# The last part of the first gate is computed before the queries instead of after the third branch projection

## The chip, the cores and the metric

One core of a Trainium2 chip runs the whole program once. The time is device microseconds (us) of one execution; the figure compared is the median of several runs of the same program. TensorE (PE) multiplies matrices into PSUM banks, VectorE (DVE) and ScalarE (ACT) read and write those banks and SBUF, GpSimd (POOL) does a few small things, and SyncE (SP) issues nearly all transfers from HBM, in one row, each waiting for its buffer.

## What is computed

A transformer block and then a second, two-layer block, on 256 tokens of width 2048. The part that the change touches is the mixing stage of the first block:

```python
mod = (c @ w_mod[l] + b_mod[l]).reshape(B, N_MOD, D)
shift_m, scale_m, gate_m = mod[:, 0, None], mod[:, 1, None], mod[:, 2, None]
...
proj = h @ w_in[l]
y_a = gmlp_spatial_gating(proj[..., COL_UV:COL_QLAT], ...)
q = apply_rope((q_lat @ w_q_up[l]).reshape(B, S, ATTN_HEADS, HEAD_DIM), cos_a, sin_a)
...
y_b = dsa_attention(q, k, v, q_idx, k_idx, idx_w)
gates = jax.nn.sigmoid(proj[..., COL_GATE:])
merged = gates[..., :D] * (y_a @ w_proj_a[l]) + gates[..., D:] * (y_b @ w_proj_b[l])
mix_out = merged @ w_out[l]
x = x + gate_m * rms_norm(mix_out, g_post_mix[l])
```

## The kernel before

Weights come in pieces of 1 MB (128 partitions x 2048 floats, tile `raw`, three buffers). Each piece is split in two halves of 1024 columns, and each half into a rounded part `wh` (line 134, ACT) and the rest `wl` (line 135, DVE), three buffers each. Every product is made of three matmuls (`mm3`; lines 144 to 146, or 211 to 213 in `linT`). A superblock of 512 output columns is 16 blocks of 128 input rows for the big weights, so four pieces. It takes two PSUM banks out of a ring of four (`acca`); the next superblock but one takes the same banks again and waits until DVE and ACT have read them.

The mixing stage runs jobs in the order of the string `ORDER`: `G` and `g` are superblocks of the first gate (tanh on ACT), `k` keys, `v` values, `S` the spatial gating, `Q` the queries, `A` starts the attention, `p0` to `p3` the four superblocks of the first branch projection, which multiply the gate by the projected branch. Behind them, outside the string, come four rounds of second gate (`w_in_g2`, four pieces) and second branch projection (`w_pb`, two pieces), and then the output projection `w_out` (function `post`, four superblocks of four pieces, `linT`).

Two kinds of side work are spread over the weight pieces. At the end of every piece `side()` runs:

```python
self.due += self.rate
while self.due >= 1 and todo:
    self.due -= 1
    self.mod_tile(new, *todo.pop(0))
for _ in range(self.pace):
    next(self.work, None)
```

`mod_tile` loads one 512 KB tile of `w_mod` (`rawm`, three buffers, line 453, issued by SP) and adds it into a running sum (`mac`, line 460, DVE). There are 96 such tiles; after each 16 a group of eight small matmuls (line 442) turns the sum into 8 columns of `mods`. `rate` is set by `r3` and `r4` in the string and is 0 ahead of `r3`. The first two groups give `gate_m`; their product with a gain, `Gm`, is turned into a row: a PE transposition (line 269), a copy on ACT (271), a store to HBM on POOL's queue (272, `grow`) and two loads that spread it over 128 partitions (275, `gr`). `work` is the attention, one head per `next`: scores (line 1024, PE), mask (1027, DVE), maximum (1043, DVE), exponentials (1044, ACT), reciprocal (1045, DVE), scaling (1047, ACT), transpositions (1054, PE), values (1030 to 1032, PE).

In `post`, each superblock's banks are released by a square on ACT (line 252) and by the product with the spread row, on DVE:

```python
done = self.nc.vector.tensor_mul(mix[h][:, c * 512:(c + 1) * 512], banks[h][q], G(c))   # line 930
```

The queries' banks are released by the rotary embedding: two copies on ACT (346, 347) and a product on DVE (350, `qT`). A scheduler turns this program into one fixed row of instructions for each engine; each engine then works through its row in order.

Of the kernel before, what the change touches and what calls it, by code (L numbers as in the profile page):

```python
# [28 lines left out]
SCALE = 128.0 ** -0.5  # L29


ORDER = "m2 m3 m4 G2 g9 g10 k0 k1 v7 v8 S r3 Q A r4 p0 p1 p2 G3 p3"

PACE = (3, 1)

# [54 lines left out]
class Kern:  # L90
# [380 lines left out]
    def block1(self, c1):  # L471
# [174 lines left out]
        def attend():  # L646
# [4 lines left out]
                "S": spatial, "Q": queries, "A": attend}  # L651
        for j in ORDER.split():
            if j[0] == "r":
# [819 lines left out]
```

## Time and profile before

| | |
|---|---|
| median of 3 runs | 2440.88 us (2440.26 to 2445.6) |
| the profiled execution | 2438.1 us, of which its span 2436.1 us |
| PE busy | 2378.1 us, 98% of the span |
| DVE busy | 1678.5 us, 69% |
| mean granted clock of PE | 0.991 |
| transfers | 540.61 MB, 222 GB/s over the span |

Busy times are sums over the whole program; they hide stages in which another engine is full. What a stage can gain or lose is read from where PE stands idle, and from what ended that idle time.

### The profile page before, as it was taken

The numbers are of one execution on the slowest core, as the hardware profiler recorded it, in microseconds if no ns is written. First come the engines' busy times: TensorE is split into PE (matmuls) and PEld (weight loads), VectorE is DVE, ScalarE is ACT, GpSimd is POOL, SyncE is SP. The second block draws the span as 40 slices with busy tenths as digits, with TensorE's granted clock in tenths as the row PEclk, the third lists the DMA queues.
The fourth block names the chain that finished last, engine by engine and source line by source line (L and its number), as shares of the span: only waits on it lengthen the run. The fifth ranks groups of instructions, "written<-read, shape, count | busy, mean of one in ns | idle before, by whom it ended". The sixth has DMA issues, their size and how long they took to land.

```text
span 2436.1 us, 37172 instructions
## 1 busy us (share of the span) xinstructions
PE 2378.1 (98%) x15142; PEld 2153.9 (88%) x15142; DVE 1678.5 (69%) x2213; ACT 1246.7 (51%) x1716; POOL 19.3 (1%) x30
## 2 busy tenths in 40 slices
PE   7999999999989999999999989999999999999997
PEld 6899989999868888888888879998898899999986
DVE  8997898888777575555556566756664477777764
ACT  5877674534464444444445454445644455554543
POOL 0000000000000000000000000000000000000000
PEclk9999999999999999999999999999999999999999
DMA  9997557999948585555555545555655544454453
GB/s 365 349 365 259 182 177 272 329 350 333 350 161 321 191 291 193 190 189 187 194 197 200 190 149 191 191 189 186 228 193 190 190 163 167 158 189 169 161 190 138
DMA packets 104043, 540.61 MB, mean 222 GB/s; under 512 B 9888, under 2 KB 18240, under 8 KB 53184
## 3 DMA queue, kind: packets, MB, share of 16 engines
q1 hardware_dynamic: 100896, 526.19, 60.8%
q10 hardware_dynamic: 2160, 8.88, 1.0%
q0 software_dynamic: 816, 3.16, 0.4%
q8 instruction: 118, 1.93, 0.3%
q14 instruction: 53, 0.43, 0.1%
HBM read 533.99 MB, written 4.21 MB: 221 GB/s over the span
## 4 chain that ended last, share of the span: by engine, by line
PE 94%; DVE 2%; ACT 1%; DMA 1%; issue 1%; POOL 0%; SPq 0%; DVEq 0%; POOLq 0%
PE acca L145 15%; PE acca L144 15%; PE acca L146 15%; PE acca L212 11%; PE acca L211 11%; PE acca L213 11%; PE acca L193 2%; PE acca L194 2%; PE acca L192 2%; PE accb L212 2%; PE accb L213 2%; PE accb L211 2%; DMA hid<-in_w_mod_dram 1%; DVE wl L135 1%; PE accb L1343 1%
## 5 line engine op out<-in xcount | busy, mean ns | idle before, releaser
L135 DVE TENSOR_TENSOR wl<-raw,wh 128x1024 fp32r<-128x1024 f32 x802 | 977.9, 1221 | 570.9 <-ACT wh L134 568.3
L134 ACT CAST wh<-raw 128x1024 fp32r<-128x1024 f32 x802 | 841.7, 1051 | 864.0 <-PE acca L213 377.9
L145 PE MATMUL acca<-Ql,wh 128*128 128x256 f32 x1024 | 290.5, 284 | 0.0
L144 PE MATMUL acca<-Qh,wh 128*128 128x256 f32 x1024 | 289.8, 284 | 0.0
L146 PE MATMUL acca<-Qh,wl 128*128 128x256 f32 x1024 | 285.5, 281 | 0.0
L212 PE MATMUL acca<-wl,Fh 128*128 128x512 f32 x704 | 276.8, 393 | 1.0 <-DVE wl L135 0.9
L213 PE MATMUL acca<-wh,Fl 128*128 128x512 f32 x704 | 275.7, 393 | 0.3 <-DVE Fl L716 0.3
L211 PE MATMUL acca<-wh,Fh 128*128 128x512 f32 x704 | 252.3, 396 | 1.7 <-ACT Fh L714 1.7
L144 PE MATMUL acca<-xh,wh 128*128 128x256 f32 x832 | 232.8, 284 | 4.5 <-ACT xh L808 3.4
L145 PE MATMUL acca<-xl,wh 128*128 128x256 f32 x832 | 233.7, 284 | 0.0
L146 PE MATMUL acca<-xh,wl 128*128 128x256 f32 x832 | 227.0, 283 | 0.0
L144 PEld LDWEIGHTS acca<-Qh,wh 128*128 128x128 f32 x1024 | 192.9, 188 | 0.5
L145 PEld LDWEIGHTS acca<-Ql,wh 128*128 128x128 f32 x1024 | 192.6, 188 | 0.8
L146 PEld LDWEIGHTS acca<-Qh,wl 128*128 128x128 f32 x1024 | 192.1, 189 | 0.4
L144 PEld LDWEIGHTS acca<-xh,wh 128*128 128x128 f32 x832 | 158.1, 190 | 7.3 <-ACT xh L808 3.6
L145 PEld LDWEIGHTS acca<-xl,wh 128*128 128x128 f32 x832 | 157.4, 189 | 1.6 <-issue 0.7
L212 PEld LDWEIGHTS acca<-wl,Fh 128*128 128x128 f32 x704 | 132.7, 189 | 29.1 <-DVE wl L135 2.2
L211 PEld LDWEIGHTS acca<-wh,Fh 128*128 128x128 f32 x704 | 131.3, 188 | 30.0 <-ACT Fh L714 2.9
L213 PEld LDWEIGHTS acca<-wh,Fl 128*128 128x128 f32 x704 | 132.4, 188 | 28.6 <-DVE Fl L716 1.5
L146 PEld LDWEIGHTS acca<-xh,wl 128*128 128x128 f32 x832 | 155.1, 190 | 1.3 <-issue 1.0
L145 PE MATMUL acca<-Al,wh 128*128 128x256 f32 x512 | 143.7, 282 | 0.0
L144 PE MATMUL acca<-Ah,wh 128*128 128x256 f32 x512 | 142.7, 281 | 0.0
(374 smaller groups left out, 4600.5 us busy)
## 6 DMA issues: line engine op xcount, KB each, us to landing
raw<-in_w_fgu_dram SPq DMA_DIRECT2D x88, 1024.0 KB, 4.8
raw<-in_w_inb_dram SPq DMA_DIRECT2D x64, 1024.0 KB, 4.8
raw<-in_w_in_dram SPq DMA_DIRECT2D x51, 1024.0 KB, 6.3
rawm<-in_w_mod_dram SPq DMA_DIRECT2D x96, 512.0 KB, 5.7
raw<-in_w_fd_dram SPq DMA_DIRECT2D x44, 1024.0 KB, 4.8
raw<-in_w_ina_dram SPq DMA_DIRECT2D x32, 1024.0 KB, 4.8
raws<-in_w_mod_dram SPq DMA_DIRECT2D x30, 1024.0 KB, 8.4
raw<-in_w_in_g_dram SPq DMA_DIRECT2D x16, 1024.0 KB, 7.2
```

What stands on the lines that cost most here:

```text
L134: nc.scalar.copy(wh[:, :per], raw[:, a:a + per])
L135: nc.vector.tensor_sub(wl[:, :per], raw[:, a:a + per], wh[:, :per].bitcast(F32))
L144: mm(out, ah, bh, start=start, stop=False, skip_group_check=True)
L145: mm(out, ah, bl, start=False, stop=False, skip_group_check=True)
L146: mm(out, al, bh, start=False, stop=stop, skip_group_check=True)
L192: mm(banks[h], xh[:, t], wh[:, s], start=fresh and k == 0, stop=False, skip_group_check=True)
L193: mm(banks[h], xh[:, t], wl[:, s], start=False, stop=False, skip_group_check=True)
L194: mm(banks[h], xl[:, t], wh[:, s], start=False, stop=k == nk - 1, skip_group_check=True)
L211: mm(banks[h][q], xh[:, t], wh[:, w], start=k == 0, stop=False, skip_group_check=True)
L212: mm(banks[h][q], xh[:, t], wl[:, w], start=False, stop=False, skip_group_check=True)
L213: mm(banks[h][q], xl[:, t], wh[:, w], start=False, stop=k == nk - 1, skip_group_check=True)
L1343: nc.tensor.matmul(ps[:, g * T:(g + 1) * T], q[g][:, P:T], kT, start=g == 0, stop=g == 1, skip_group_check=True)
```

## The change

One job of the order string moves: `G3`, the last superblock of the first gate (four pieces, 192 matmuls of 256 columns), from behind `p2` to behind `S`. No instruction is added or removed.

```diff
-ORDER = "m2 m3 m4 G2 g9 g10 k0 k1 v7 v8 S r3 Q A r4 p0 p1 p2 G3 p3"
+ORDER = "m2 m3 m4 G2 g9 g10 k0 k1 v7 v8 S G3 r3 Q A r4 p0 p1 p2 p3"
```

What else moves follows from the string: `G3` now stands where `rate` is 0 and no attention is running. Before, its four pieces had `rate` 4 and one head each.

**Behind the queries, DVE.** `wl` are weight halves, `yal` the rest of the gated branch, `qT<-acca` releases a queries' bank. Before:

```order
L135 TENSOR_TENSOR wl<-raw,wh 128x1024
L351 TENSOR_TENSOR sw<-sw,sinr 128x512
L337 TENSOR_TENSOR yal<-sv,yah 128x512
L135 TENSOR_TENSOR wl<-raw,wh 128x1024
L1096 SCALAR_TENSOR_TENSOR sv<-sv,u 128x512
L460 SCALAR_TENSOR_TENSOR mac<-rawm,vec,mac 128x1024
L350 TENSOR_TENSOR qT<-acca,cosr 128x512 x3
```

DVE at the same work now:

```order
L1096 SCALAR_TENSOR_TENSOR sv<-sv,u 128x512 x2
L135 TENSOR_TENSOR wl<-raw,wh 128x1024
L337 TENSOR_TENSOR yal<-sv,yah 128x512 x2
L135 TENSOR_TENSOR wl<-raw,wh 128x1024 x5
L350 TENSOR_TENSOR qT<-acca,cosr 128x512
L351 TENSOR_TENSOR sw<-sw,sinr 128x512
L135 TENSOR_TENSOR wl<-raw,wh 128x1024
L352 TENSOR_TENSOR qT<-qT,sw 128x512
L350 TENSOR_TENSOR qT<-acca,cosr 128x512
```

The rest of the spatial gating (`sv`, `yal`) and the tile sum (line 460) no longer stand among or right ahead of the releases.

**In the output projection, PE.** `acca_6710` and `acca_6711` are the banks of its first superblock, `acca_6858` and `acca_6859` of its second, `acca_7002` of its third, which is the ring's first pair again. Before:

```order
L211 MATMUL acca_6711<-wh_6816,xh_93 128x512
L442 MATMUL accb_5529<-cst_84,rawm_5522 128x1 x8
L269 MATMUL accb_6695<-cst_84,Gm_89 16x128
L212 MATMUL acca_6710<-wl_6817,xh_93 128x512
...
L211 MATMUL acca_6858<-wh_6862,xh_93 128x512
...
L211 MATMUL acca_7002<-wh_7006,xh_93 128x512
```

PE there now:

```order
L211 MATMUL acca_6859<-wh_6946,xh_93 128x512
L442 MATMUL accb_5767<-cst_84,rawm_5760 128x1 x8
L269 MATMUL accb_6695<-cst_84,Gm_89 16x128
L212 MATMUL acca_6858<-wl_6947,xh_93 128x512
...
L211 MATMUL acca_7002<-wh_7006,xh_93 128x512
```

The transposition of the gate row (line 269) follows the fifth group of tiles in both; between it and the third superblock stood 118 matmuls of 512 columns, and now stand 34.

**The same place on DVE.** `mix` (line 930) releases the banks, `mac` adds a tile. Before:

```order
L460 SCALAR_TENSOR_TENSOR mac<-rawm,vec,mac 128x1024
L135 TENSOR_TENSOR wl<-raw,wh 128x1024 x2
L930 TENSOR_TENSOR mix_6705<-acca,gr_6700 128x512
L930 TENSOR_TENSOR mix_6706<-acca,gr_6700 128x512
L135 TENSOR_TENSOR wl<-raw,wh 128x1024
L460 SCALAR_TENSOR_TENSOR mac<-rawm,vec,mac 128x1024 x2
L135 TENSOR_TENSOR wl<-raw,wh 128x1024
```

DVE there now:

```order
L135 TENSOR_TENSOR wl<-raw,wh 128x1024
L460 SCALAR_TENSOR_TENSOR mac<-rawm,vec,mac 128x1024 x3
L930 TENSOR_TENSOR mix_6705<-acca,gr_6700 128x512
L930 TENSOR_TENSOR mix_6706<-acca,gr_6700 128x512
L930 TENSOR_TENSOR mix_6705<-acca,gr_6700 128x512
L930 TENSOR_TENSOR mix_6706<-acca,gr_6700 128x512
L460 SCALAR_TENSOR_TENSOR mac<-rawm,vec,mac 128x1024 x5
```

Three tile sums stand right ahead of the first release, and the releases of both superblocks stand together.

**The same place on SP.** The loads of the output projection's pieces and of the tiles. Before:

```order
L130 DMA raw<-in_w_out_dram 128x2048
L453 DMA rawm<-in_w_mod_dram 128x1024
L130 DMA raw<-in_w_out_dram 128x2048
L453 DMA rawm<-in_w_mod_dram 128x1024 x2
L130 DMA raw<-in_w_out_dram 128x2048
L453 DMA rawm<-in_w_mod_dram 128x1024
L130 DMA raw<-in_w_out_dram 128x2048
```

SP there now; the single `raw` in the third and fifth rows are the 11th and the 12th of the 16 pieces:

```order
L130 DMA raw<-in_w_out_dram 128x2048 x2
L453 DMA rawm<-in_w_mod_dram 128x1024 x2
L130 DMA raw<-in_w_out_dram 128x2048
L453 DMA rawm<-in_w_mod_dram 128x1024
L130 DMA raw<-in_w_out_dram 128x2048
L453 DMA rawm<-in_w_mod_dram 128x1024 x9
L130 DMA raw<-in_w_out_dram 128x2048
```

Nine tile loads stand in one run behind the 12th piece. The first of the nine is the tile that the third of DVE's three sums (above) adds.

## Rows read from the trace of the kernel before

**Rows 1.** The page's first part: busy time of each engine.

```profile
PE 2378.1 (98%) x15142; PEld 2153.9 (88%) x15142; DVE 1678.5 (69%) x2213; ACT 1246.7 (51%) x1716; POOL 19.3 (1%) x30
```

**Rows 2.** PE's waits from 335 to 485 us: total, times, longest.

```profile
PE acca L144 <- DVE qT L350: 6.7, 1, 6.7
```

**Rows 3.** Timeline of PE from 361 to 374 us: start, duration, instruction.

```profile
362.32 0.28 PE L145 MATMUL acca<-qll,wh 128*128 128x256 f32 x1
362.44 0.28 PE L146 MATMUL acca<-qlh,wl 128*128 128x256 f32 x1
369.38 0.55 PE L144 MATMUL acca<-yah,wh 128*128 128x256 f32 x1 [6.66 <-DVE qT L350]
...
373.79 0.33 PE L144 MATMUL acca<-yah,wh 128*128 128x256 f32 x1
```

**Rows 4.** Stretches of 5 us: length, PE busy, granted clock, transfer share, GB/s.

```profile
365.00:370.00 5.00, 0.62 (x3) 0.71 0.76 252
370.00:375.00 5.00, 5.00 (x29) 0.61 0.61 202
375.00:380.00 5.00, 5.00 (x43) 1.00 0.63 182
```

**Rows 5.** Timeline of DVE at the first release of the queries.

```profile
367.36 1.28 DVE L460 SCALAR_TENSOR_TENSOR mac<-rawm,vec,mac 128x1024 f32<-128x1024 f32 x1
368.56 1.88 DVE L350 TENSOR_TENSOR qT<-acca,cosr 128x512 f32<-128x512 f32 x3
```

**Rows 6.** Stretches of 40 us: PE, weight load, DVE, ACT, POOL busy; clock, transfers.

```profile
340.00:380.00 40.00, 33.34 (x233) 31.68 (x232) 39.32 (x61) 21.46 (x31) 0.00 (x0) 0.91 0.59 198
...
620.00:660.00 40.00, 40.00 (x178) 33.16 (x177) 31.84 (x30) 17.15 (x21) 1.10 (x2) 1.00 0.94 339
```

**Rows 7.** The gate row: instructions on it (duration, first and last start).

```profile
L269 PE MATMUL accb<-cst,Gm x1: 269/269/269, 614.1 to 614.1; 128*16 128x128 f32 x1
...
L271 ACT COPY gT<-accb x1: 255/255/255, 614.5 to 614.5; 16x128 f32<-16x128 f32 x1
...
L275 POOL DMA_DIRECT2D gr<-grow x2: 537/550/562, 621.1 to 621.8; - x2
L272 POOL DMA_DIRECT2D grow<-gT x1: 661/661/661, 615.0 to 615.0; - x1
...
DMA to landing us min/median/max: 5.5/7.2/8.0
```

**Rows 8.** Timeline of DVE at the first releases of the output projection.

```profile
635.31 1.28 DVE L930 TENSOR_TENSOR mix<-acca,gr 128x512 f32<-128x512 f32 x2
636.89 1.22 DVE L135 TENSOR_TENSOR wl<-raw,wh 128x1024 fp32r<-128x1024 f32 x1 [0.30 <-ACT wh L134]
638.03 2.60 DVE L460 SCALAR_TENSOR_TENSOR mac<-rawm,vec,mac 128x1024 f32<-128x1024 f32 x2
```

**Rows 9.** Timeline of PE in the output projection.

```profile
636.05 0.39 PE L212 MATMUL acca<-wl,xh 128*128 128x512 f32 x1
636.28 0.39 PE L213 MATMUL acca<-wh,xo 128*128 128x512 f32 x1
```

**Rows 10.** Timeline of SP: issues in the output projection.

```profile
630.91 0.33 SPq L130 DMA_DIRECT2D raw<-in_w_out_dram  x1
632.11 0.33 SPq L453 DMA_DIRECT2D rawm<-in_w_mod_dram  x1
...
641.79 0.33 SPq L130 DMA_DIRECT2D raw<-in_w_out_dram  x1
```

**Rows 11.** The tiles from 470 to 700 us: issue to landing, 54 of them.

```profile
DMA to landing us min/median/max: 3.6/6.0/9.2
```

**Rows 12.** Timelines of DVE and PE: pieces of one attention head and what stands between.

```profile
458.00 0.55 DVE L1027 SCALAR_TENSOR_TENSOR e<-accb,sc 128x384 f32<-128x384 f32 x1
...
461.94 0.60 DVE L1043 TENSOR_REDUCE mx<-e 128x1 f32<-128x128 f32 x2
...
464.79 0.15 DVE L1045 RECIPROCAL sm<-sm 128x2 f32<-128x2 f32 x1
...
375.48 0.82 PE L1024 MATMUL accb<-kT,qT 128*128 128x128 f32 x4
```

## The prediction

> **What bounds the kernel now.** PE is busy for 98% of the span [rows 1], so I first looked for the places where it is not. PE's waits over the stretch that the change touches show one [rows 2]: 6.7 us, for DVE's first reading of a queries' bank. The timeline [rows 3] puts it between the last matmul of the queries at 362.44 and the first of `p0` at 369.38. The first branch projection takes the ring's banks from the queries, and the release (line 350) stands on DVE behind a tile sum at 367.36 [rows 5]; DVE is full around it, 39.3 of 40 us [rows 6]. The wait costs more than itself. PE's granted clock is 0.61 over the 5 us after it [rows 4], and 20 steps of matmuls take from 369.38 to 373.79, so 0.22 us each, where they took 0.12 before it [rows 3]: 4.4 us instead of 2.4, another 2.0 us. From there to the end of the output projection the view by stretches has PE busy throughout, while the transfers are near their limit, as in its row from 620 to 660 us: PE 40 of 40 us, transfer share 0.94 [rows 6]. So the rest has no idle time to win, but it has little spare room in the transfers either.
>
> **The change, step by step.** The work is the same; 192 matmuls of 256 columns, eight splits on ACT and DVE, and four 1 MB loads move. On PE, DVE and ACT this alone costs nothing, since the sums stay the same. What counts is what no longer waits, and what becomes late.
>
> *The wait behind the queries.* `G3` gives PE 192 matmuls of 0.12 us, some 23 us, between the gating and the queries. In them DVE has eight splits to do of the new work, spaced by some 1.14 us, so 9 us; the other 14 us take in the rest of the gating. DVE's new order agrees: ahead of the first release stand only weight halves, which are limited by their buffers and not by DVE. From the end of the queries' first superblock PE has another 48 matmuls, 5.7 us, before it needs the bank; DVE has two releases, one split, two more rotary operations to do until the second bank is free too, about 4.5 us with the copies on ACT. So the wait goes: **-6.7 us**, and with it the slow clock: **-2.0 us**. If the cover of 5.7 us should be missed, the wait is the difference, 0 to 1 us.
>
> *The attention.* The eight heads had twelve pieces and now have eight until `p3` ends, so they run into the second gate's first rounds. In PE's new row the last two heads stand close to the second branch projection that needs them. From the last head's scores to the next weight half on which PE waits, DVE's new row holds one mask, two maxima, one reciprocal, four tile sums and two weight halves. Spaced as the rows show (0.47, 0.52, 0.07, 1.2 and 1.14 each [rows 5, 8, 12]) that is 8.1 us, behind 0.8 us of scores, 8.9 in all. PE has 36 weight matmuls of 0.12 us in it and twelve small ones of the heads, at most 0.2 each as the scores show [rows 12], so 6.4 to 6.7 us. Difference: about **+2.5 us**. If every tile lands in time and ACT is quick the wait can vanish (0); if DVE has to wait for one tile by another 1.5 us, it is 4.
>
> *The gate row.* This is where I expect the gain to go. `G3` had `rate` 4: four pieces issued 16 of the 96 tiles. At its new place `rate` is 0, so all later tiles are 16 behind, a whole group. The transposition of the gate row (line 269) stands right behind the fifth group in PE's row, before and now, so it slides back: 118 matmuls stood between it and the third superblock of the output projection, now 34 do. At 0.23 us each [rows 9] the time from it to that superblock shrinks from 26.8 to 7.7 us. The row itself needs longer [rows 7]: transposition at 614.1, copy at 614.5, store issued at 615.0 and 5.5 us to landing, the two loads issued at 621.1 and 621.8, and 7.2 and 8.0 us to landing. That is 14.2 us to the first half of the row, and 0.6 us more for the first release. Before, the two releases began at 635.31 and ended 1.3 us later [rows 8], four us ahead of their need at 614.1 + 26.8 = 640.9. Now PE waits for the bank at least 14.2 + 0.6 - 7.7 = **7.1 us**, by these rows.
>
> The release has a second reason to be late, on DVE and SP. Ahead of it now stand three tile sums. The third tile is the first of nine that SP issues behind the 12th piece. The 12th piece needs the buffer of the 9th, whose second half can be split only when PE is nearly through the second superblock: in the trace the 12th is issued at 641.79, 0.9 us after that superblock's end at 640.9 [rows 10]. So, counted from the moment at which PE is ready for the third superblock: 0.9 us to the 12th piece, 1.2 us to the tile behind it (630.91 to 632.11 [rows 10]), 6.0 us to its landing (the median of 54 tiles of this stretch [rows 11]), 1.2 for the sum, 0.6 for the release, 0.1 for the matmul to start (an estimate): 10.0 us. With the quickest and the slowest tile, 3.6 and 9.2 us [rows 11], it is 7.6 and 13.2. The later of the two reasons decides, so **+10.0 us**, and after a wait longer than the one at 362 us PE runs slowly again: **+2.0 us**, as above.
>
> The page "DMA: Bandwidth & Descriptors" of the Trainium skill (section on the anatomy of one DMA) fits a transfer as about 2 us plus its bytes at 436 GB/s, from another issuing path; for 512 KB this is an estimate of 3.2 us. The trace has 6.0 in this stretch, with transfers queued behind each other, and no tile under 3.6; by the page the wait would be set by the gate row, 7.1 us, and the sum 2.9 us lower than below.
>
> Behind the wait nothing further should be late: eight tiles stand ahead of the 13th piece, but PE then has the third superblock, 96 matmuls or 21.8 us, already loaded, and DVE needs 1.2 us for each tile. The last group of tiles ends no later than before, since the string's later pieces take up the rest.
>
> *The sum.* -6.7 - 2.0 + 2.5 + 10.0 + 2.0 = +5.8 us. On the profiled execution, 2438.1 us, this is 2443.9; that execution lies 2.8 us below the median of 2440.88, so the median should come to 2446.7, say **2447 us**.
>
> **The rivals.**
>
> *The gate row comes in time (faster).* The wait at the queries goes, and none takes its place. For it: the row's transfers are small, and before they had four us to spare. Against it: the 34 matmuls of cover are in PE's fixed row, and the chain of 14.2 us is nearly all transfers on a busy queue [rows 7]; both they and the tile would have to land within about 7 us less. The cover decides from 7.7 us on. Time: 2440.9 - 8.7 + 2.5 = 2435, down to 2432 without the wait in the attention.
>
> *A short wait (no change).* The tile lands in 3.6 us and the gate row sets the wait: 7.1 us. For it: PE stands still meanwhile, so fewer pieces are drawn and the transfers are freer than the median shows. Against it: SP has just issued a full 1 MB piece ahead of the tile. Time: 2440.9 + 5.8 - 2.9 = 2444.
>
> *A long wait.* The tile lands as the slowest did, 9.2 us, or the five sums behind the release hold up the next weight half as well. For it: nine tiles in one run at a transfer share of 0.94. Against it: only one 1 MB piece and one or two tiles are ahead of it in the queue. Time: 2440.9 + 5.8 + 3.2 = 2450, to 2456 if two or three of the later tiles hold up the splits by 1.5 to 2 us each.
>
> *The change does not do what it says.* `p0` waits as before, since `yal` or the queries' releases are still late on DVE. Against it: DVE's order above, and 14 us of room. Time: 2447 + 8.7 = 2456.
>
> **How the numbers follow.** A measurement of this kernel can tell about 0.2%, 4.9 us, from no change. The forecast, a wait of 8 to 12 us in the output projection, has 0.55, and gives 2444 to 2450; three quarters of that lie above 2445.8. The long wait has 0.14, the short one 0.18, no wait 0.09, and the change without effect 0.04. Slower by over 0.2%: 0.42 + 0.14 + 0.04 = 0.60. Within 0.2%: 0.13 + 0.18 = 0.31. Faster: 0.09. The range goes from 2438 (the short wait with none in the attention, 2441, and a little of the faster case) to 2456 (the long wait). The likeliest case's own range is 2444 to 2450.
>
> **What would show it.** In the changed trace: no wait of PE at `p0`, and a granted clock of 1.0 there (step 1); waits of one or two us for weight halves near the first pieces of the second branch projection (step 2); a single wait of about 10 us of an L211 on `acca` in the output projection, ended by line 930 or 252, with line 269 only 34 matmuls ahead of it and a tile's landing just before the release (step 3); a clock near 0.6 behind it (step 4). If line 930 waits for `gr` and not for the tile sum, the gate row alone set the wait. The forecast is wrong if the release comes within 8 us of the transposition, or if the splits behind it starve PE a second time.

## The result and the profile after

| | before | after |
|---|---|---|
| median | 2442.9 us (2440.3 to 2445.6, 6 runs) | 2456.8 us (2449.2 to 2460.6, 6 runs) |
| ratio | | 1.0058 [1.0047, 1.0069] |
| the profiled execution, span | 2436.1 us | 2454.8 us |

The change makes the kernel 0.58% slower, about 14 us, where 6 were forecast and 2456 was the range's end. The profiled execution of before is a quick one, nearly 5 us below its median; the 18.7 us between the two spans are therefore more than the change costs.

The first part of the page of after: as many instructions on every engine as before [rows 1]; PE is busy for 4.9 us longer, at a mean granted clock of 0.989 instead of 0.991.

```profile
PE 2383.0 (97%) x15142; PEld 2155.8 (88%) x15142; DVE 1678.8 (68%) x2213; ACT 1247.2 (51%) x1716; POOL 19.3 (1%) x30
```

PE's waits from 335 to 485 us. The wait of 6.7 us for the queries' bank is gone; two others for weight halves stand at the end of the stretch [rows 2].

```profile
PE acca L146 <- DVE wl L135: 3.4, 1, 3.4
PE acca L144 <- ACT wh L134: 0.6, 1, 0.6
```

Stretches of 5 us of after, with the columns of [rows 6] (PE, weight load, DVE, ACT and POOL busy, granted clock, transfer share, GB/s). The first branch projection starts at 385.5: full work, full clock, where [rows 4] had 0.62 of 5 us and a clock of 0.61 to 0.71. The middle pair is the end of the attention, the last three the output projection.

```profile
385.00:390.00 5.00, 5.00 (x43) 4.95 (x43) 5.00 (x8) 3.68 (x5) 0.00 (x0) 1.00 0.60 161
475.00:480.00 5.00, 1.59 (x12) 1.40 (x13) 2.91 (x5) 0.77 (x3) 0.00 (x0) 1.00 0.74 270
480.00:485.00 5.00, 4.41 (x24) 4.18 (x24) 4.21 (x6) 2.99 (x8) 0.00 (x0) 0.66 0.71 220
645.00:650.00 5.00, 0.00 (x0) 0.00 (x0) 0.90 (x1) 0.00 (x0) 0.00 (x0) 0.50 1.01 419
650.00:655.00 5.00, 2.92 (x7) 2.37 (x8) 4.92 (x7) 0.00 (x0) 0.00 (x0) 0.50 0.61 221
655.00:660.00 5.00, 5.00 (x17) 3.94 (x17) 3.81 (x3) 0.00 (x0) 0.00 (x0) 0.72 0.75 226
```

PE's timeline at that place. The third superblock stands still for 12.0 us behind line 930, and the matmuls then come every 0.43 us instead of the 0.23 of [rows 9]; 13 of them do, 13 x 0.2 = 2.6 us. The granted clock of 0.50 in the rows above is the lower of its two levels (1.2 and 2.4 GHz).

```profile
639.68 0.39 PE L213 MATMUL acca<-wh,xo 128*128 128x512 f32 x1
652.08 0.76 PE L211 MATMUL acca<-wh,xh 128*128 128x512 f32 x1 [12.01 <-DVE mix L930]
652.64 0.63 PE L212 MATMUL acca<-wl,xh 128*128 128x512 f32 x1
653.07 0.63 PE L213 MATMUL acca<-wh,xo 128*128 128x512 f32 x1
```

The gate row of after [rows 7]: transposition 17.9 us later than before, the loads 19.2 us later.

```profile
L269 PE MATMUL accb<-cst,Gm x1: 269/269/269, 632.0 to 632.0; 128*16 128x128 f32 x1
...
L275 POOL DMA_DIRECT2D gr<-grow x2: 537/550/562, 640.3 to 641.0; - x2
...
DMA to landing us min/median/max: 4.6/6.5/8.3
```

SP's issues, and DVE at the release of after [rows 8, 10]. The piece goes out at 641.09, the tile behind it at 642.28; its sum starts when it lands, at 650.05, and the release stands behind that sum. The row's first half, which this release reads, landed 4.6 us after its issue at 640.3, at 644.9, and the second by 641.0 + 8.3 = 649.3: the tile was the later of the two.

```profile
641.09 0.33 SPq L130 DMA_DIRECT2D raw<-in_w_out_dram  x1
642.28 17.87 SPq L453 DMA_DIRECT2D rawm<-in_w_mod_dram  x8
```

```profile
650.05 1.28 DVE L460 SCALAR_TENSOR_TENSOR mac<-rawm,vec,mac 128x1024 f32<-128x1024 f32 x1 [4.14 <-DMA rawm<-in_w_mod_dram]
651.25 2.48 DVE L930 TENSOR_TENSOR mix<-acca,gr 128x512 f32<-128x512 f32 x4
```

DVE near the last head. The weight half at 478.43, on which PE waits 3.4 us, stands behind a tile sum that waits 2.1 us for its load.

```profile
474.58 0.56 DVE L1027 SCALAR_TENSOR_TENSOR e<-accb,sc 128x384 f32<-128x384 f32 x1 [1.51 <-PE accb L1024]
477.23 1.28 DVE L460 SCALAR_TENSOR_TENSOR mac<-rawm,vec,mac 128x1024 f32<-128x1024 f32 x1 [2.09 <-DMA rawm<-in_w_mod_dram]
478.43 1.22 DVE L135 TENSOR_TENSOR wl<-raw,wh 128x1024 fp32r<-128x1024 f32 x1
```

To see where time goes, five points of PE's row are compared, read as first or last starts from the views of single tiles: the last key, value or gate matmul ahead of the spatial gating's end (line 193), the last matmul of the second branch projection (146 on `ybh`), the last of the output projection (212 on `xh`), and the first that reads the normed rows (211 on `Fh`). All programs do the same weight matmuls between two points. "Start" is the first point; programs with the same code up to there show 351.2 to 354.3 us, and the tied ones (below; runs 6, 8, 12, 13, 15, 16), which load no tile ahead of 329 us, 347.7 to 350.9.

| program | ratio to before | start | gating to end of second branch | output projection | norm chain |
|---|---|---|---|---|---|
| before | | 351.2 | 244.8 | 89.9 | 9.9 |
| after | 1.0058 | 351.5 | 242.9 | 106.3 | 10.4 |
| 1 tiles late | 1.0015 [1.0006, 1.0025] | 353.7 | 244.3 | 95.2 | 9.8 |
| 3 row early | 1.0008 [0.9999, 1.0017] | 353.7 | 241.0 | 88.5 | 16.0 |
| 4 behind queries | 0.9999 [0.9990, 1.0007] | 351.7 | 246.7 | 90.4 | 9.9 |
| 5 after again | 1.0051 [1.0039, 1.0063] | 353.9 | 241.1 | 104.9 | 10.4 |
| 6 rate 4, tied | 1.0085 [1.0071, 1.0098] | 350.9 | 268.9 | 88.6 | 10.4 |
| 7 row early, pace 2 | 1.0020 [1.0011, 1.0028] | 353.8 | 239.8 | 90.3 | 27.7 |
| 8 row early, rate 2, tied | 1.0026 [1.0017, 1.0036] | 350.1 | 258.3 | 90.3 | 10.4 |
| 10 heads late | 1.0063 [1.0049, 1.0076] | 354.3 | 260.3 | 88.5 | 10.4 |
| 11 both late | 1.0003 [0.9994, 1.0012] | 353.1 | 244.4 | 89.9 | 9.9 |
| 12 after, tied | 1.0038 [1.0027, 1.0050] | 347.7 | 244.8 | 104.5 | 10.8 |
| 13 rates 2 and 3, row early | 0.9995 [0.9986, 1.0004] | 348.7 | 248.4 | 88.6 | 11.5 |
| 14 few tiles by heads | 1.0100 [1.0086, 1.0114] | 353.1 | 238.7 | 120.9 | 10.4 |
| 15 rate 3, tied, row early | 1.0014 [1.0006, 1.0023] | 349.0 | 255.4 | 90.6 | 9.8 |
| 16 rates 2 and 3, row late | 1.0009 [1.0000, 1.0018] | 349.5 | 244.7 | 95.3 | 9.8 |

With the wait gone and nothing else, the column behind "start" would be 244.8 - 8.7 = 236.1; after has 6.8 us more (below, a run's loss in the attention is its value less 236.1), and its output projection takes 16.4 us more than before. (Runs 2 and 9 put other work ahead of the first point and are told below.)

### The profile page after: what moved, and what is told of

It is laid out like the page before. It is cut to its first block, busy times and chain, and to the rows that moved or that the text cites. A ratio compares the mean times of both kernels' runs of the same rounds, so it can differ in the third digit from the quotient of the medians.

```text
span 2454.8 us, 37167 instructions
## 1 busy us (share of the span) xinstructions
PE 2383.0 (97%) x15142; PEld 2155.8 (88%) x15142; DVE 1678.8 (68%) x2213; ACT 1247.2 (51%) x1716; POOL 19.3 (1%) x30
## 4 chain that ended last, share of the span: by engine, by line
PE 91%; DMA 3%; DVE 3%; ACT 2%; issue 1%; POOL 0%; SPq 0%; DVEq 0%; ACTq 0%; POOLq 0%
PE acca L145 15%; PE acca L144 15%; PE acca L146 14%; PE acca L212 11%; PE acca L213 11%; PE acca L211 11%; PE acca L193 2%; PE acca L194 2%; PE acca L192 2%; PE accb L213 2%; PE accb L212 2%; PE accb L211 2%; DMA rawm<-in_w_mod_dram 2%; DMA hid<-in_w_mod_dram 1%; DVE wl L135 1%
```

## The experiments

### Do the terms come again? Run 5

The changed kernel once more.

> The changed kernel a second time, for the spread of its terms between two profiles. If the terms read from its first profile belong to the kernel, the second one has them again: no wait behind the queries, 3 to 4 us of waits for weight halves near 480 us, about 7 us more than before from the first matmul of the first branch projection to the last of the second, a wait of an L211 of 11 to 13 us in the output projection; 2454 to 2459. If parts of it were chance (the 1.9 us of waits near 790 us, the tile that VectorE waits for near 476 us), those are the parts that differ.

2455.1 us against 2442.6. No wait at the queries, 11.7 us at line 930, 7.6 in the norm chain: these belong to the kernel. Of PE's waits from 335 to 800 us:

```profile
PE acca L211 <- DVE mix L930: 11.7, 1, 11.7
PE acca L146 <- DVE wl L135: 3.2, 3, 1.5
PE acca L144 <- ACT wh L134: 0.6, 1, 0.6
```

The attention's loss is 241.1 - 236.1 = 5.0 us here: four waits of 0.4 to 1.5 us for weight halves between 478 and 499 us, 3.8 us in all, at a clock of 1.0. In after two waits make 4.0 us, and the clock of 0.66 behind the first (row 480 to 485) takes another (1 - 0.66) x 5 = 1.7 us; that names 5.7 of 6.8. About 1.2 us of the loss has no name in either profile. The tile on which DVE waited 2.1 us in after comes 0.2 us late in run 5, so the longer first wait and its slow clock were chance, and the rest was not. The waits near 790 us (1.9 us in after) are not there again, and the stretch from the norm chain to the second gate row takes 486.3 us as in before, where the first profile had 489.5: 3 us of the first comparison were chance.

### What do the 16 postponed tiles cost? Runs 1, 11 and 10

Three kernels with the order of before, in which only side work is held back during `G3`. `h0` and `h1` set the heads' `pace`.

```diff
-... p0 p1 p2 G3 p3
+... p0 p1 p2 r0 G3 r4 p3          (run 1: tiles)
+... p0 p1 p2 h0 G3 h1 p3          (run 10: heads)
+... p0 p1 p2 h0 r0 G3 h1 r4 p3    (run 11: both)
```

> The kernel before, with the gate's last superblock where it was, but with rate 0 during it and 4 again behind it: only the 16 tiles are postponed, the order of the weight pieces is unchanged. If the postponed tiles are what the output projection waits for, the wait behind the queries stays (6.7 us) and a wait of an L211 on acca of 8 to 12 us appears, with 2 to 3 us of slow clock behind it: 10 to 15 us slower than before, 2453 to 2458. If the place of the superblock is what costs (its crowding of the heads, its splits), this kernel has none of that: 2443, no difference. If both are needed, a wait of 2 to 6 us: 2445 to 2449.

> The kernel before in its order, but no step of the attention is taken during the last gate superblock; the heads have eight pieces, as in the changed kernel, and the tiles are as before. If the 5 to 7 us lost between the first and the second branch projection in the changed kernel come from the heads alone, they show here in the same place, with the wait behind the queries still there: 2448 to 2450. If it takes the postponed tiles beside the heads, nothing or up to 2 us is lost: 2443 to 2445.

> The kernel before in its order, but neither steps of the attention nor tiles during the last gate superblock: all that the changed kernel postpones, without the cover behind the queries. If the losses of the changed kernel come from what is postponed and the gain from the cover (8.7 us), this is the changed kernel plus that gain: 2463 to 2467. If they come from the superblock's new place, this is like the run with the tiles late alone: 2445 to 2449. In between, the new place makes the part of the loss that is missing.

Run 1 costs 3.8 us, with a wait of 3.1 us at line 930: the small outcome. Its transposition of the gate row comes at 624.3, 10 us later than before, 2.5 of them by its later start.

```profile
PE acca L211 <- DVE mix L930: 3.1, 1, 3.1
```

Run 11 costs nothing, against both theories, and its trace says why: on every engine its row of instructions is that of before, one by one, by operation, shape and tile name (2213 on DVE, 578 loads on SP, 15142 matmuls). The edit changed the program and not what the scheduler made of it, so run 11 is the kernel before, measured again, and tests nothing about late tiles. By the string the tiles written ahead of the last head are 6 + 8 x 4 = 38 in before, in run 11 and in the changed kernel, 54 in run 10 and 30 in run 1. So empty places in the string alone need not move a load; where the edit moves heads and tiles against each other, as in run 1, the tiles do come late.

In after the row of loads is late for another reason: it starts late. SP had issued 80 tiles by 600 us in before and 76 in after, and by 400 us 20 against 14. In after no tile goes out between 242 and 385 us, in before the loads start again at 362.6. The first row is before from 340 to 380 us, the second after from 380 to 400:

```profile
L453 SPq DMA_DIRECT2D rawm<-in_w_mod_dram x5: 328/328/328, 362.6 to 377.7; - x5
L453 SPq DMA_DIRECT2D rawm<-in_w_mod_dram x4: 327/328/328, 385.6 to 399.3; - x4
```

Run 10 is the surprise: 14 us slower, all of it between gating and second branch, and slower than either outcome had it. Its only difference from run 11, and so from before, is that the last two heads are written behind 16 more tiles. Line 1026 (the heads' scores; 1024 before) of run 11, then of run 10, first and last start:

```profile
L1026 PE MATMUL accb<-kT,qT x32: 272/368/382, 377.0 to 456.4; 128*128 128x128 f32 x16, 128*128 128x256 f32 x16
```

```profile
L1026 PE MATMUL accb<-kT,qT x32: 272/368/382, 378.2 to 503.6; 128*128 128x128 f32 x16, 128*128 128x256 f32 x16
```

The last head's mask comes at 459.2 with 27 tile sums done ahead of it on DVE (counted from 355 us), in run 10 at 504.8 with 43. So a head on DVE stands behind the tile sums that were written ahead of it; a sum whose load is late holds up all behind it (2.1 us in after, above; 0.2 to 0.9 us at several sums of run 10), and the heads go at the pace of the loads. The Trainium skill says as much of the queue ("PSUM — Partial Sum Buffer", section on engine and sequencer instructions: the queues of ScalarE, VectorE and GpSimd are strictly first in, first out); by that rule a head can't pass a sum that waits, and the traces agree: in after the weight half at 478.43 and then the last head's maxima come only behind the sum that waited 2.1 us.

### Fewer tile sums ahead of the heads: runs 14 and 7

Run 14 is the changed kernel with `r2` for `r4` and `r6` behind `p3`; run 7 has the gate row early (below) and `PACE = (3, 2)`.

```diff
-... S G3 r3 Q A r4 p0 p1 p2 p3
+... S G3 r3 Q A r2 p0 p1 p2 p3 r6   (run 14)
```

> The changed kernel with rate 2 during the four branch pieces and 6 behind them: on VectorE the last head stands behind 25 tile sums instead of 34, the first output release behind 85 as before. If the heads are late because they stand behind tile sums, the last head's scores come 15 us or more earlier than in the changed kernel (470 to 475 us there) and the 5 to 7 us in the attention fall to 0 to 2. The tiles come no sooner, so the wait in the output projection stays at 12 us or grows: 2450 to 2462. If VectorE or the last heads' own chain sets the loss, the last head is not earlier.

> The third experiment (row early) with two steps of the attention for each weight piece instead of one, so that the eight heads are done after half as many pieces. If the 5 to 7 us that are lost between the first and the second branch projection come from the heads having too few pieces, they vanish: 2438 to 2442. If VectorE and the transfers are short there whatever the heads do, nothing is gained there: 2444 to 2448. The last group of tiles already ended 6 us too late in the third experiment (a wait of 8.7 us behind the output projection); if the heads at twice the pace push tiles back further, that wait grows and takes the gain: 2446 to 2456.

The last head's mask is at 465.1 behind 17 sums in run 14 and at 469.1 behind 21 in run 7; in after it is at 474.6 behind 26. The loss falls to 238.7 - 236.1 = 2.6 and to 3.7 us, and not to the 0 to 2 and the nothing that were expected; the last scores of run 14 come 12.5 us earlier than in after, where 15 were expected. Both pay later: run 14 waits 11.3 us at line 930 and 10.2 us for a group's sum in the output projection and comes to 2466.0 us, over its range; run 7 waits 20.3 us for the last group behind it (2448.1, its third outcome). In run 14 the release at line 930 waits for the gate row itself, whose transposition is at 651.0:

```profile
PE acca L211 <- DVE mix L930: 11.3, 1, 11.3
PE accb L442 <- DVE rawm L460: 10.2, 1, 10.2
661.88 2.48 DVE L930 TENSOR_TENSOR mix<-acca,gr 128x512 f32<-128x512 f32 x4 [1.77 <-DMA gr<-grow]
```

### The gate row: runs 3 and 16

In run 3 the row is written ahead of the second round of the second gate; run 16 is told below.

```diff
         for s in range(4):
+            if s == 1:
+                nc.vector.tensor_mul(self.Gm, self.mods[:, 32:48], ...)
+                self.row_out(0, self.Gm)
+                grow = [...]
+                for i in range(2):
+                    self.row_in(0, grow[i], i * 1024, 1024)
             gt = []
...
-        nc.vector.tensor_mul(self.Gm, self.mods[:, 32:48], ...)
-        self.row_out(0, self.Gm)
...
```

> The changed kernel, with the gate row's transposition, store and loads written ahead of the second superblock of the second branch projection instead of behind the last. The tiles stay postponed. If the gate row is what makes the first release late (by its landing, or because it puts the release behind tile sums on VectorE), the wait of 12.0 us in the output projection is gone: 2442 to 2445. If the tile sums ahead of the release decide, as the prediction held, a wait of 8 to 12 us stays and the time is within 4 us of the changed kernel's 2456.8.

2445.0 us: the wait of 12.0 us is gone, and with it 16 to 18 us of the output projection. The transposition comes at 516.9, where after has it at 632.0. It isn't the row's landing alone: on DVE the release stands behind 76 tile sums, where it has 86 ahead of it in after and 85 in before (all sums from the first on), and it runs at 617.67 instead of 651.25. So my account "tile sums decide" is right only for the row of instructions that the late gate row had brought about. The late tiles come out at the end instead: 16.0 us of norm chain, with PE waiting for the last group's sum.

```profile
PE accb L442 <- DVE rawm L460: 8.7, 1, 8.7
```

### Is it the place? Runs 4 and 9

```diff
+... v7 v8 S r3 Q A r4 G3 p0 p1 p2 p3         (run 4)
+... m4 g9 g10 k0 k1 v7 v8 S G2 r3 Q A r4 p0 p1 p2 G3 p3   (run 9)
```

> The superblock stands behind the queries and the start of the attention instead of ahead of the queries, with rate 4: tiles and heads have as many pieces before the second gate as in the kernel before. By the prediction's account the wait behind the queries is not covered here (the superblock's own first bank is released by the queries), so 6 to 8 us of wait move to line 144's first bank of the superblock, the heads have their twelve pieces, and the output projection does not wait: 2443, within 0.2% of before. If it is the earlier place as such that costs in the attention or in the output projection, it is 5 to 15 us slower: 2448 to 2458.

> The kernel before, with the gate's third superblock (the one that stands ahead of the eleven closing pieces, with no tiles and no heads in it) put between the gating and the queries in place of the last one, which stays behind the third branch projection. If the changed kernel is slow because the last superblock took four pieces' worth of heads and 16 tiles away from behind the third branch projection, this one keeps the gain of the cover (8.7 us) and has none of the losses: 2434 to 2437, faster than both. If any superblock between the gating and the queries costs in the attention or in the output projection, it is like the changed kernel: 2450 to 2457. If the closing pieces and the gating miss the cover that this superblock gave them, a new wait shows ahead of or in the gating (before 350 us) and takes 3 to 9 us back: 2437 to 2444.

Run 4 is equal to before: the 6.7 us move to the superblock's own first bank, as forecast, and neither heads nor tiles meet PE sooner. Its waits from 340 to 460 us:

```profile
PE acca L144 <- DVE qT L350: 6.7, 1, 6.7
PE acca L146 <- DVE wl L135: 2.0, 1, 2.0
```

Run 9 gains the cover and loses it: 2444.7 against 2442.9. DVE works without a pause from 365 to 396 us there, the first head's mask comes at 395.9 instead of 378.2, and the second branch ends at 600.0 instead of 596.0 though the first branch begins 2.2 us sooner. The third outcome, at another place than I had named.

### Tiles beside the moved superblock: runs 2, 6, 12, 8, 15, 13 and 16

All have `G3` at the new place, and all but run 12 a rate during it. In all but run 2 each tile's load is tied behind the weight load written ahead of it:

```diff
             while self.due >= 1 and todo:
                 self.due -= 1
-                self.mod_tile(new, *todo.pop(0))
+                with tc.issue_after(self.load.ins):
+                    self.mod_tile(new, *todo.pop(0))
```

```diff
+... S r4 G3 r3 Q A r4 p0 p1 p2 p3      (runs 2 and 6)
+... S r2 G3 r3 Q A r4 p0 p1 p2 p3      (run 8, row early)
+... S r3 G3 Q A p0 p1 p2 p3 r4         (run 15, row early)
+... S r2 G3 r3 Q A r3 p0 p1 p2 p3 r4   (run 13, row early; run 16, row late)
```

> The changed kernel with rate 4 during the moved superblock: the tiles are no longer postponed against before (16 of them are drawn even earlier). If the postponed tiles cause the wait in the output projection, that wait (12.0 us and 2.7 us of slow clock) is gone, the wait behind the queries stays away, and what remains is the attention's loss of about 7 us against a gain of 8.6: 2440 to 2444, 13 to 16 us below the changed kernel. If the place of the superblock costs by itself, the wait or another of its size stays: 2452 to 2457. A third possibility: the tiles crowd the transfers ahead of the queries and a new wait of 2 to 5 us shows there: 2443 to 2449.

> Rate 4 during the moved superblock as in the second experiment, and each tile's load is issued only after the weight load that was emitted ahead of it, so that the tiles cannot be drawn forward to 240 us. The wait in the output projection should be gone as in the second experiment, and the 10 us that were lost ahead of 340 us too. If the second experiment was slow because its tiles were drawn forward, this one comes to 2443 to 2447, 10 to 14 us below it. If the tiles cost the same wherever they lie beside the moved superblock and the heads, the loss turns up in the attention (10 us or more from the first branch projection to the end of the second) and the time stays at 2452 to 2458.

> The changed kernel with each tile's load tied behind the weight load emitted ahead of it and nothing else, as a control for the two runs with tied tiles. If the tie itself was what cost 15 to 25 us in the attention there, it does so here too: 2465 to 2480. If the tiles beside the moved superblock were the cost, this one is like the changed kernel: 2453 to 2459.

> The third experiment with rate 2 during the moved superblock, each tile's load tied behind the weight load that was emitted ahead of it. The last group of tiles is 8 tiles less late. If the wait of 8.7 us behind the output projection in the third experiment was the postponed tiles coming out at the end, it falls back to the 6.5 to 7.6 us that line 729 has there before and after, and 3 to 6 us come back: 2438 to 2442, which would be faster than both. If the tiles beside the moved superblock cost as much in the attention as they win behind the output projection: 2443 to 2447.

> The eighth run (row early, tied tiles, rate 2 during the moved superblock) with rate 3 instead of 4 during the four branch pieces and 4 again behind them. On VectorE the last head then stands behind 37 tile sums instead of 46, while the tiles start some 20 us earlier than in the changed kernel. If the attention's loss comes from the heads' places behind tile sums, it falls from 22 us to 0 to 4, the output projection does not wait, and the gain of the cover is left: 2436 to 2441, faster than before. If tied tiles between the weight loads cost there by themselves, 10 us or more stay: 2446 to 2452.

> As the run with rates 2 and 3, but rate 3 from the moved superblock on: the last head stands behind 40 tile sums, with 4 tiles more during the superblock. If the places behind tile sums decide, it lies between that run and the eighth: some us slower than the first, 2438 to 2445. If tied tiles cost by themselves: 2446 to 2452.

> The run with rates 2 and 3, with the gate row written where the changed kernel has it, behind the second gate. If it is the tiles' lag that made the gate row late, the tiles that start 20 us earlier are enough, the wait in the output projection is 0 to 3 us, and the time is within 3 us of the run with the row early: 2437 to 2443. If the row is late wherever it is written there, the wait of 8 to 12 us and its slow clock are back: 2448 to 2454.

Run 2 (2457.5, ratio 1.0058) has no wait in the output projection, 88.6 us, and is as slow as after. The scheduler drew 18 of its tiles forward to places ahead of 340 us, where before has 10, and its first point comes at 364.0 instead of 351.2; tied, in run 6, it is back at 350.9. PE's stretch from 240 to 260 of run 2, then of before:

```profile
240.00:260.00 20.00, 11.16 (x68) 9.94 (x67) 13.42 (x17) 6.47 (x11) 1.61 (x1) 0.74 0.69 234
240.00:260.00 20.00, 16.99 (x137) 16.06 (x136) 13.51 (x22) 11.78 (x19) 1.72 (x1) 1.00 0.60 205
```

The tied runs show what tiles cost beside the heads. Run 12, tied and otherwise as after, has a loss of 8.7 us, so the tie does not make the 22 and 33 us of runs 8 and 6. Those two came out slower than either of their outcomes (2449.7 and 2463.9 us). Along with the changed kernel's own family:

| program | tile sums ahead of the last head, from 355 us | its mask, us behind the gating | loss in the attention |
|---|---|---|---|
| 14 | 17 | 112.0 | 2.6 |
| 7 | 21 | 115.3 | 3.7 |
| 3, 5, after | 26 | 122.7 to 123.1 | 4.9, 5.0, 6.8 |
| 16, 13 | 33 | 126.2 | 8.6, 12.3 |
| 12 | 35 | 129.4 | 8.7 |
| 15 | 36 | 135.7 | 19.3 |
| 8 | 42 | 146.1 | 22.2 |
| 6 | 48 | 158.3 | 32.8 |

On the whole, the later the last head, the larger the loss; run 12 is out of order, later than run 13 and with less loss. Runs 13 and 16 differ by 3.7 us at the same place of the heads, and the clock makes most of it: in run 13 two rows of 5 us have 0.66, 2 x 0.34 x 5 = 3.4 us, and in run 16 the same rows have 1.00. First the two rows of run 13, then those of run 16:

```profile
480.00:485.00 5.00, 4.53 (x24) 4.13 (x24) 4.06 (x6) 2.00 (x4) 0.00 (x0) 0.66 0.88 298
490.00:495.00 5.00, 3.62 (x17) 3.62 (x18) 4.85 (x5) 0.00 (x0) 0.00 (x0) 0.66 0.66 198
480.00:485.00 5.00, 3.81 (x30) 3.57 (x31) 4.92 (x6) 2.23 (x4) 0.00 (x0) 1.00 0.78 283
490.00:495.00 5.00, 3.34 (x28) 3.35 (x29) 5.00 (x5) 0.00 (x0) 0.00 (x0) 1.00 0.61 179
```

So a difference of 2 to 4 us between two rows of the table can be the clock alone. Run 13's loss was forecast as 0 to 4 us and is 12.3, 3.4 of it clock; run 8, with nine sums more, has 22.2, so the sums are a large part of it and not all. Run 15 lies between the two, as its first outcome had it, but over that range, at the lower end of the second (2446.3 us). Run 13 is the best of the new place, 2440.2 against 2440.9, 0.9995 [0.9986, 1.0004]: no difference from before. That is not the place's doing alone: behind the first point it takes 3.9 us more than before (348.5 against 344.6 over the three columns), and it starts 2.5 us earlier; every tied run starts ahead of every untied one. The order of before with tied tiles was not run, so how much the tie wins by itself is not shown. Run 16 (2443.8 us, just over its range) has the row late and loads tiles during `G3`, from 330 us on, where after loads none between 242 and 385: a wait of 3.1 us at line 930, where run 12, tied too, has 11.3. So most of that wait is the tiles' lag. Run 12, then run 16:

```profile
PE acca L211 <- DVE mix L931: 11.3, 1, 11.3
PE acca L211 <- DVE mix L931: 3.1, 1, 3.1
```

## Why the prediction was wrong

*The wait behind the queries* (-6.7 and -2.0): right. PE's first matmul of the first branch stands 34.0 us behind the gating instead of 18.1; `G3` is 192 x 0.118 = 22.6 us of it, so 6.7 us were won there, and the clock of 1.0 behind it gives the rest.

*The attention* (+2.5): right in kind, too small by half. 5.0 and 6.8 us in two profiles, where 4 was the upper bound. The step that failed is that the sum had one wait at one weight half, with the tile sums at 1.2 us each as if every tile had landed, and neither further waits nor a slow clock. In after the first wait is 3.4 us, since DVE waits 2.1 us for a tile (the sentence "if DVE has to wait for one tile by another 1.5 us, it is 4" saw that), and a clock of 0.66 behind it takes 1.7. In run 5 the tile is only 0.2 us late and the first wait is 1.5, less than the forecast; three more of 0.4 to 1.3 us behind it make 3.8. It also looked at the last heads alone, while all eight go at the loads' pace (run 10 against 11, run 14). And the heads did not need twelve pieces before: eight heads, one for each piece, end by the string with the second of `G3`'s four. In after as many sums stand ahead of the last head as before, 26 against 27 from 355 us on; they start 23 us later.

*The gate row* (+10.0 and +2.0): right in place, mechanism and order of the two reasons, too small in size. The transposition is at 632.0, and the second superblock's last matmul starts at 639.7, so PE was ready for the third at 639.9: 7.9 us, where the forecast had 7.7. From there 1.2 us passed to the piece, 1.2 to the tile, 7.8 to its landing, 1.2 for the sum, 0.8 to PE: 12.2, where the forecast had 10.0. The mis-sized term is the landing, 6.0 us assumed and 7.8 measured, in a stretch with a transfer share of 1.01. By the page "DMA: Bandwidth & Descriptors" of the Trainium skill (section on the anatomy of one DMA) the estimate was 3.2; the measurement decides. The gate row's first half landed at 644.9; alone it would have made a wait of about 644.9 + 0.6 + 0.8 - 639.9 = 6.4 us (an estimate), near the 7.1 of the forecast. The slow clock is 2.6 us instead of 2.0. The stage is 15.0 and 16.4 us longer in the two profiles instead of 12.0; 12.0 + 0.6 of a following wait, which the sum did not have, + 2.6 name 15.2 of it.

Two places of the forecast do not fit its own sum. With the quickest tile, 3.6 us, the tile's path takes 7.6 us, so the short wait of 7.1, which the gate row was to set, could not come of that tile. With the 3.2 us estimated from that page of the Trainium skill it takes 7.2, so there too the tile and not the gate row would have set the wait. Neither changes the result.

*"16 tiles behind, a whole group"*: wrong as a count. From 400 to 640 us SP is 3 to 8 tiles behind. The first load behind the queries comes 23.0 us later than before, and the 70th to the 80th load still come 15 to 17 us later; why they do not catch up is not shown. Nor is the rate of 0 during `G3` shown as the cause: run 11 has it without late tiles, run 1 has it with a wait of 3.1 us. The slide of the transposition was read from PE's row and came out right all the same, by luck as far as its reason goes.

*"Behind the wait nothing further should be late"*: nearly. One wait of 0.6 us for a weight half follows and the norm chain is 0.5 us longer; 3 us more of the first profile did not come again.

Added up on the second profile: -3.7 from the gating to the second branch (-8.7 + 5.0), +15.0, +0.5, so +11.8 us; the medians are 12.5 and 13.9 apart. The forecast had -6.2 + 12.0 = +5.8. The rival that came nearest is the long wait; I gave it 0.14 and ended the range with it at 2456, and 2456.8 was measured. What came was no rival but the forecast's own two terms, one near its upper bound (12.0 of 13.2) and one beyond it (5.0 and 6.8 over 4).

Shown by runs: the cover's gain (after and run 5, against run 4), the gate row (3), the tiles' lag that makes it late (16 against 12), the heads behind tile sums (10 against 11, 14). Open: about 1.2 us of the attention's loss, why the late loads do not catch up, what the tie wins in the order of before, and whether any order keeps the 8.7 us; run 13 got within the measurement of before and not below it.

## What to carry to other kernels

Before work is moved ahead of a stream of loads, ask what else goes at that stream's pace: here the heads and the gate row stood behind tile sums on DVE, and 23 us of PE work taken from beside the loads made both meet PE earlier than the loads could. A place in the program is no time: find the n-th load in the trace, not the n-th place in the loop, and compare the rows of instructions first, for an edit can leave them as they were (run 11). And where a wait is the sum of steps on a queue at a share near 1, take the upper half of the landing times, not the median: the two tiles on this chain took 7.8 and 7.4 us, where the median was 6.0.

## What the hardware showed beside that

Three single waits of 3.1 to 3.4 us were followed by matmuls at the lower level of the clock: in after (the wait until 479.7), in run 1 (until 646.8) and in run 16 (until 642.9). The shares are means over 5 us, so they are added: 0.66 in after from 480 to 485 (above) and in run 1 from 645 to 650, and 0.84 and 0.82 in run 16 from 640 to 650. Each comes to 1.7 us of full clock, (1 - 0.66) x 5 and (0.16 + 0.18) x 5. Run 1, then the two rows of run 16:

```profile
645.00:650.00 5.00, 3.23 (x8) 2.64 (x9) 4.96 (x7) 0.35 (x2) 0.00 (x0) 0.66 0.86 344
640.00:645.00 5.00, 2.08 (x6) 1.74 (x7) 4.76 (x7) 1.50 (x3) 0.00 (x0) 0.84 1.02 427
645.00:650.00 5.00, 5.00 (x19) 4.03 (x19) 2.04 (x2) 0.00 (x0) 0.00 (x0) 0.82 0.85 271
```

The length of a wait does not tell what it costs in clock, though. Run 16 waits 3.3 us at one matmul of the second branch and its clock stays at 1.00 there; run 13 waits 2.4 us at the same matmul and has 0.66 (both rows 490 to 495 above). Run 13, then run 16:

```profile
491.38 0.51 PE L145 MATMUL acca<-ybl,wh 128*128 128x256 f32 x1 [2.38 <-DVE ybl L337]
491.66 0.39 PE L145 MATMUL acca<-ybl,wh 128*128 128x256 f32 x1 [3.26 <-DVE ybl L337]
```

Three waits of 1.5, 0.6 and 0.4 us between 478 and 486 us, in run 5, left it at 1.0, at the place where after fell to 0.66:

```profile
475.00:480.00 5.00, 3.34 (x24) 2.62 (x22) 3.27 (x7) 2.55 (x5) 0.00 (x0) 1.00 0.84 294
480.00:485.00 5.00, 4.37 (x33) 3.81 (x33) 4.96 (x7) 3.20 (x9) 0.00 (x0) 1.00 0.71 217
```

So two profiles of one kernel can differ by 1.7 us in a stage by the clock alone, as after and run 5 do, and whoever prices a wait of 2 to 3 us has to allow for either level behind it. What decides between them is not shown here.
